# Order of the work between gate and MLP in a fused S5, gate and MLP block on one Trainium2 core

## Chip, cores, metric

One of the cores of a Trainium2 chip runs the whole program; nothing is sent to another core. The metric is device time of one execution in microseconds (us), the median of several runs. TensorE (PE) does the matrix products, VectorE (DVE), ScalarE (ACT) and GpSimd (POOL) the elementwise work, and the queue of SyncE (SP) starts most transfers. Each engine works through its own instructions strictly in program order and waits for the others by semaphores.

## What is computed

One layer on 1024 latent tokens with 1024 channels (and 256 context tokens): modulated RMS norm, a bidirectional state-space mixer, a gate, a second modulated RMS norm, an MLP with squared ReLU, and a last RMS norm. The part at issue begins behind the mixer:

```python
z = gelu(mixer_out)                         # (1024, 1024)
x = x + g1 * (z * sigmoid(z @ glu_w + glu_b))
h = rmsnorm(x, norm2_g) * (1 + sc2) + sh2
a = relu(h @ mlp_w1 + mlp_b1)
x = x + g2 * ((a * a) @ mlp_w2 + mlp_b2)
out = rmsnorm(x, final_g)
```

## The kernel before

**Layout.** Channels lie on the 128 partitions, tokens along the free dimension. The 1024 channels are eight tiles, the 1024 tokens two halves of 512 (`halves`, `hf` 0 and 1). Every operand of a product is kept as two roundings, a high part and a rest (`z[:, 0]`, `z[:, 1]`; the pairs of `put`, `rounded` and `rest`), and a product is three matmuls (`mm3`, L770 to 773). A high part is a copy on ACT (`S.copy`); the rest is a subtraction on DVE or POOL. `T`, `UT`, `W`, `A` and `G2` (`GW`, `G` in the rows) are SBUF tensors; `bank(i)` is a PSUM bank of 512 columns.

**Gate.** `gate(b, d, hf, k)` accumulates eight channel tiles k into the gate of output tile d and half hf. `gate_outs(units, hf, sq, eng, ahead)` (L969 to 981) finishes a list of (tile, bank) units: `z_sum` (L944) adds high part and rest of z on POOL into a buffer, `gate_out` (L949) applies the sigmoid (ACT, L951), multiplies with that buffer (DVE, L952) and adds the result to the residual `acc` (DVE, L953), and `sum_sq` (L960) squares `acc` (ACT, L966) and adds the square to the running sum `ss` (L967; on POOL, or on DVE in the last call). The sums and squares go to buffers that `tmp()` takes in turn from `ring`, seven of the eight `places`; `ahead` says how many z sums are issued in advance.

**First norm.** While the gate of half 1 runs on PE, the norm of half 0 is taken. `norm_cols` (L985) sums `ss` over the partitions on PE (L990) and forms one reciprocal root per token with a root on ACT (L994) between four-element work on DVE (L993 to L1002); `norm_rows` (L1004) spreads it over the partitions on PE (L1008). `norm2` (L1011) then makes z of the second product stage in place: a multiplication (DVE, L1016), scale and shift (ACT, L1017), the high part (ACT, L1024) and the rest (L1027, engine `eng`). Program order at this place: the units (6, 7) of half 0, four `put_w1_half` (ACT L917, DVE L918), the units 0 and 1 of half 1 (L1050), the column sums of the first norm behind the second product of tile 3 (L1056), and the row products behind the second product of tile 4 (L1061). The last call of `gate_outs` (L1069) finishes tiles 2 to 7 of half 1.

**First MLP product.** `h @ w1` is done by seven products instead of eight for each two by two block of quarter operands. `L` lists the 112 products (block b, number i), PE takes them in that order, and `pbank` gives their banks. The operand of the weights is made by `sum1` (L1105; a sum or difference of parts of w1, on POOL for the first blocks), `round1` (ACT, L1111 through L925) and `rest1` (L1115 through L922); for i = 6 `rest1` also starts the load of a later block of w1. `slot(p)` is one of eight slots, so operand p can be rounded only when product p - 8 has read its own. The operand of the tokens is `zop[i]`: quarters of z and the combinations T1, T2, T3, T4, called `t1`, `t2`, `zop[4]` (made in place) and `t4`. PE adds and subtracts quarters with unit matrices into four banks (`z_diff`, L1267), DVE adds more in place (`u2`, L1296 and L1303), and `put` splits them.

`step1(p)` (L1183) issues product p, the first part of what follows it (`after1`, L1150), the rounding of operand p + 5, the output of a finished tile (ACT L1137 and L1138, then a store to DRAM), the rest of operand p + 5 and the sum of operand p + 6; step 0 makes only that last sum. Products 0 to 5 need only half 0 and weights that are ready; the second norm (half 1) lies among them: `norm_cols` behind step 1, `norm_rows` behind step 3, and `norm2_second` ahead of step 5, with its rests on POOL (L1027). So in the program the column sums come behind product 1, product 4 comes behind `norm_rows`, and its copy out of PSUM (ACT, L1160) ahead of the first L1017 of the second norm. Then follow T1, T2, step 6 (with operand 11, the first of the second block), and in one loop over the four tiles T3's split and the two additions that make T4.

The order is written out by hand; each engine's order is the program's.

Of the kernel before, what the change touches and what calls it, by code (L numbers as in the profile page):

```python
# [7 lines left out]
F32 = mybir.dt.float32  # L8
F32R = mybir.dt.float32r
AF = mybir.ActivationFunctionType  # L10
OP = mybir.AluOpType
# [36 lines left out]
def kernel(ctx, tc, cst, bc, x, xl, ada_w, glu_w, w1, w2, out):  # L48
    nc = tc.nc
    V, S, P, PE, SP = nc.vector, nc.scalar, nc.gpsimd, nc.tensor, nc.sync  # L50
# [17 lines left out]
    def vw(ap, *dims):  # L68

        if len(dims) == 1:  # L70
            return ap
        names = "abcdef"[:len(dims)]
        return ap.rearrange("p (%s) -> p %s" % (" ".join(names), " ".join(names)),
                            **{names[i]: dims[i] for i in range(len(dims))})

    def size(dims):
        n = 1
        for d in dims:
            n *= d
        return n  # L80

    def at(tile_, off, *dims):
        return vw(tile_[:, off:off + size(dims)], *dims)

    def sb(off, *dims):
        assert R3 + off + size(dims) <= R3 + NR3
        return at(T, R3 + off, *dims)

    def bank(i, n=512, o=0):
        return PS[:, 512 * i + o:512 * i + o + n]  # L90
# [547 lines left out]
    def slot(i):  # L638
        return CT[:, :, :, 0, i] if i < 14 else LT[:, :, :, 0, i - 14]
# [32 lines left out]
    for q in range(1, 40):  # L672
# [23 lines left out]
        for hf in range(2):  # L696
            p = slot(2 * q - 1)[:, 32 * hf:32 * hf + 32]
# [12 lines left out]
    def zt(j):  # L710
        return vw(zs[j][:, :], 2, 1024)
# [179 lines left out]
    places = [sb(10240 + 512 * i, 512) for i in range(3)] + [at(UT, 512 * i, 512) for i in range(5)]  # L891
    ring = places[:7]
    nt = [0]

    def tmp():
        nt[0] += 1
        return ring[nt[0] % len(ring)]
# [17 lines left out]
    def put(to, src, eng=V, *dims):  # L915
        hi, lo = (vw(v[:, 0:size(dims)], *dims) for v in to) if dims else to
        S.copy(hi, src)  # L917
        eng.tensor_tensor(lo, src, hi.bitcast(F32), op=OP.subtract)  # L918
# [5 lines left out]
    def rounded(to, src, *dims):  # L924
        S.copy(vw(to[0][:, 0:size(dims)], *dims) if dims else to[0], src)  # L925
# [6 lines left out]
    def load_w1(b):  # L932
        SP.dma_start(out=vw(raw1(b), 8, 256), in_=w1v[:, :, 256 * b:256 * b + 256])
# [5 lines left out]
    def put_w1_half(b, kh, p):  # L939
        put(slot(p), vw(raw[0], 2, 2, 4, 128)[:, b % 2, kh], V, 4, 128)  # L940

    zf = {}

    def z_sum(d, hf):  # L944
        z = zt(d).bitcast(F32)
        zf[d, hf] = tmp()
        P.tensor_tensor(zf[d, hf], z[:, 0, halves[hf]], z[:, 1, halves[hf]], op=OP.add)

    def gate_out(b, d, hf):  # L949
        o = acc[:, d, halves[hf]]  # L950
        S.activation(b, b, AF.Sigmoid, bias=C("glub")[:, d:d + 1])  # L951
        V.tensor_tensor(b, zf[d, hf], b, op=OP.mult)  # L952
        V.scalar_tensor_tensor(o, b, g1[:, d:d + 1], o, op0=OP.mult, op1=OP.add)  # L953
# [6 lines left out]
    def sum_sq(d, toks, eng=None):  # L960
        n, ss = toks.stop - toks.start, sq_sum(toks)
        if d == 0:
            S.activation(ss, acc[:, d, toks], AF.Square)
        else:
            sq = tmp()[:, 0:n]
            S.activation(sq, acc[:, d, toks], AF.Square)  # L966
            (eng or P).tensor_tensor(ss, ss, sq, op=OP.add)  # L967

    def gate_outs(units, hf, sq=True, eng=None, ahead=1):  # L969

        for u in units[:ahead]:
            z_sum(u[0], hf)
        for i in range(len(units) + 1):
            if i + ahead < len(units):
                z_sum(units[i + ahead][0], hf)
            if i < len(units):
                gate_out(bank(units[i][1]), units[i][0], hf)
            if units[i:] == [(7, 3)]:
                S.activation(warm, one, AF.Sqrt)
            if i and sq:  # L980
                sum_sq(units[i - 1][0], halves[hf], eng)
# [22 lines left out]
    def norm_rows(r, b, toks=halves[0]):  # L1004

        n = toks.stop - toks.start
        for c in range(n // 128):
            PE.matmul(bank(b, 128, 128 * c), r[:, c:c + 1].to_broadcast([128, 128]), ident, start=True, stop=True)  # L1008
        return bank(b, n)

    def norm2(ds, hf, rb, eng=V):  # L1011
        hs_, xn = halves[hf], {}

        def first(d):
            xn[d] = tmp()
            V.tensor_tensor(xn[d], acc[:, d, hs_], rb, op=OP.mult)  # L1016
            S.activation(xn[d], xn[d], AF.Identity, scale=a2[:, d:d + 1], bias=sh2[:, d:d + 1])  # L1017

        for d in ds[:2]:
            first(d)  # L1020
        for d in ds:
            yield
            z = zt(d)
            S.copy(z[:, 0, hs_], xn[d])  # L1024
            if d + 2 in ds:
                first(d + 2)
            eng.tensor_tensor(z[:, 1, hs_], xn[d], z[:, 0, hs_].bitcast(F32), op=OP.subtract)  # L1027

    def add_b2(hf):
        for d in range(8):  # L1030
# [13 lines left out]
            gate(bank(b), d, 0, k)  # L1044
    gate_outs([(6, 0), (7, 2)], 0)
    G2 = sp.tile([128, 1024], F32, name="G2", tag="gw")
    for p, (b, kh) in enumerate(((0, 0), (1, 0), (0, 1), (1, 1))):
        put_w1_half(b, kh, p)
    load_w1_half(2)
# [7 lines left out]
    for d, b in ((4, 6), (5, 7), (6, 1), (7, 3)):  # L1057
        for k in range(8):
            gate(bank(b), d, 1, k)
            if (d, k) == (4, 1):  # L1060
                rb = norm_rows(r_, 2)  # L1061
# [4 lines left out]
                for kh in range(2):  # L1066
                    put_w1_half(2, kh, 4 + kh)
                load_w1(0)
    gate_outs([(2, 4), (3, 5), (4, 6), (5, 7), (6, 1), (7, 3)], 1, eng=V, ahead=4)  # L1069

# [4 lines left out]
    def zh(k, hf):  # L1077
        z = zt(k)
        return z[:, 0, halves[hf]], z[:, 1, halves[hf]]

    t1, t2, t4 = ([(at(W, o + 1024 * k, 512), at(W, o + 1024 * k + 512, 512)) for k in range(4)] for o in (0, 4096, 8192))
    zop = [[zh(k, 0) for k in range(4)], t1, t2, [zh(4 + k, 1) for k in range(4)], [zh(k, 1) for k in range(4)],
           [zh(4 + k, 0) for k in range(4)], t4]
# [6 lines left out]
    def pbank(p):  # L1090
        return bank((4, 6, 0, 2, 3, 0)[p] if p < 6 else (2, 3, 1, 0, 5, 7, 4, 6)[(p - 6) % 8])
# [3 lines left out]
    def operand(p):  # L1095
        b, i = L[p]
        w = vw(raw1(b), 2, 4, 256)
        a11, a12, a21, a22 = (w[:, kh, :, 128 * f:128 * f + 128] for f in range(2) for kh in range(2))
        s2 = at(G2, 0, 4, 128)
        return (a11, a21, s2, a21, s2, a12, a22)[i], {1: (a21, a22), 2: (a21, a11), 3: (a12, s2), 4: (a22, s2)}.get(i)  # L1100

    def eng1(p):
        return P if p < POS[2, 1] else V

    def sum1(p):  # L1105
        if p < len(L):
            o, ab = operand(p)
            if ab:
                eng1(p).tensor_tensor(o, *ab, op=OP.add if L[p][1] == 1 else OP.subtract)

    def round1(p):  # L1111
        if p < len(L):
            rounded(slot(p), operand(p)[0], 4, 128)

    def rest1(p):  # L1115
        if p < len(L):
            b, i = L[p]
            rest(slot(p), operand(p)[0], eng1(p), 4, 128)
            if i == 6:
                if b == 0:  # L1120
                    load_w1(1)
                elif b < 14:
                    load_w1(b + 2)
                else:
                    load_w2(b - 14)

    def product1(p):
        b, i = L[p]
        hi, lo = (vw(v, 4, 128) for v in slot(p))
        for k in range(4):  # L1130
            mm3(pbank(p), (hi[:, k], lo[:, k]), zop[i][k], k == 0, k == 3)
# [9 lines left out]

    yp = [places[n] for n in (0, 1, 2, 7)] + [at(G2, 512, 512)]

# [37 lines left out]
        yield  # L1181

    def step1(p):  # L1183
        product1(p)
        a = after1(p)
        next(a)
        if p > 0:
            round1(p + 5)
        next(a, 0)
        if p > 0:  # L1190
            rest1(p + 5)
        if p == 7:
            load_w1(2)
        sum1(p + 6)


    UNITS = [[2 * u, 2 * u + 1] for u in range(7)] + [[14], [15]]
# [67 lines left out]
    sums = [bank(i) for i in (5, 7, 4, 6)]  # L1265
# [4 lines left out]
            PE.matmul(sums[k], w, v, start=n == 0, stop=n == 3)  # L1270

    def norm2_second(ks):
        for _ in norm2(ks, 1, rb, P):
            pass

    S.copy(unit[:, 0], ident)
    S.activation(unit[:, 1], ident, AF.Identity, scale=-1.0)
    ring = places[3:7]
    for p in range(6):
        if p == 5:  # L1280
            norm2_second(range(4))
            for k in range(4):
                z_diff(k, zop[4][k], zop[0][k])
            norm2_second(range(4, 8))
            for k in range(4):
                put(t1[k], sums[k])
        step1(p)
        if p == 1:
            r_, *_ = norm_cols(7)
        elif p == 3:  # L1290
            rb = norm_rows(r_, 1)
# [4 lines left out]
            V.tensor_tensor(u2[k], zop[0][k][n].bitcast(F32), u2[k] if n else sums[k], op=OP.add)  # L1296
    for k in range(4):
        put(t2[k], u2[k])
    step1(6)
    for k in range(4):  # L1300
        put(zop[4][k], sums[k])
        for n in range(2):
            V.tensor_tensor(u2[k], zop[5][k][n].bitcast(F32), u2[k], op=(OP.subtract, OP.add)[n])  # L1303
    for k in range(4):
        put(t4[k], u2[k])
    for p in range(7, len(L)):
        b, i = L[p]
# [7 lines left out]
    for u in range(8):  # L1315
        bs = UNITS[u]
        for t in range(16):
            hf, d = t // 8, t % 8
# [45 lines left out]
    ring = ring[:3]  # L1364
# [5 lines left out]
    for d in range(8):  # L1370
# [4 lines left out]
        if d == 5:  # L1375
            rb = norm_rows(r_, 2, first)
# [8 lines left out]
    rb = norm_rows(r_, 3, toks[0])  # L1385
# [12 lines left out]
    rb = norm_rows(r_, 2, toks[1])  # L1398
# [66 lines left out]
```

## Time and profile before

| what | value |
|---|---|
| runs | 1132.06, 1131.56, 1127.25 us; median 1131.56 |
| profiled execution | 1133.16 us, span 1131.4 us |
| PE busy | 988.6 us, 87% of the span |
| DVE, ACT, POOL busy | 779.7, 498.2, 311.8 us |
| TensorE clock granted, mean | 0.936 of full speed |

A busy share is an average over stages with different limits; the stretch of the change lies from 384 to 484 us of the span. A timeline row gives start, length, engine, line, operation, output and inputs, count, and in brackets how long the engine had been idle and what released it.

### The profile page before, as it was taken

The numbers are of one execution on the slowest core, as the hardware profiler recorded it, in microseconds if no ns is written. First come the engines' busy times: TensorE is split into PE (matmuls) and PEld (weight loads), VectorE is DVE, ScalarE is ACT, GpSimd is POOL, SyncE is SP. The second block draws the span as 40 slices with busy tenths as digits, with TensorE's granted clock in tenths as the row PEclk, the third lists the DMA queues.
The fourth block names the chain that finished last, engine by engine and source line by source line (L and its number), as shares of the span: only waits on it lengthen the run. The fifth ranks groups of instructions, "written<-read, shape, count | busy, mean of one in ns | idle before, by whom it ended". The sixth has DMA issues, their size and how long they took to land.

```text
span 1131.4 us, 14742 instructions
## 1 busy us (share of the span) xinstructions
PE 988.6 (87%) x5424; PEld 815.2 (72%) x5424; DVE 779.7 (69%) x1290; ACT 498.2 (44%) x923; POOL 311.8 (28%) x251
## 2 busy tenths in 40 slices
PE   3568676646889997899999999989999999999996
PEld 3337565525878875688888888868888888888885
DVE  8999999999975685775656565656454454454377
ACT  7147474335973566555565655453202202201113
POOL 2787999807562635420000000000000000000003
PEclk9779798867899998899999999999999999999998
DMA  9414355494677410152333232346132232320104
GB/s 383 168 38 147 118 166 136 94 253 133 209 229 243 156 56 19 47 177 99 118 103 119 103 122 103 121 166 243 66 112 90 97 112 75 112 94 19 38 0 149
DMA packets 79032, 142.33 MB, mean 126 GB/s; under 512 B 5744, under 2 KB 44656, under 8 KB 77808
## 3 DMA queue, kind: packets, MB, share of 16 engines
q1 hardware_dynamic: 74528, 126.71, 33.8%
q10 hardware_dynamic: 4432, 14.68, 3.9%
q8 instruction: 42, 0.69, 0.3%
q14 instruction: 30, 0.25, 0.1%
HBM read 106.77 MB, written 34.60 MB: 125 GB/s over the span
## 4 chain that ended last, share of the span: by engine, by line
PE 58%; DVE 23%; DMA 7%; ACT 5%; issue 4%; POOL 2%; SPq 1%; ACTq 0%; DVEq 0%; POOLq 0%
PE PS L771 18%; PE PS L772 18%; PE PS L773 18%; DMA DY<-X 2%; DVE X L468 2%; DVE X L467 2%; DVE PS L466 1%; DVE PS L465 1%; DVE X L449 1%; DVE PS L698 1%; DMA T<-DY 1%; DVE PS L952 1%; DVE UT L700 1%; DVE UT L967 1%; DMA KD<-T 1%
## 5 line engine op out<-in xcount | busy, mean ns | idle before, releaser
L1328 DVE SCALAR_TENSOR_TENSOR T<-PS,T 128x512 f32<-128x512 f32 x128 | 96.1, 751 | 164.5 <-PE PS L773 164.5
L967 POOL TENSOR_TENSOR T<-T,UT 128x256 f32<-128x256 f32 x14 | 10.3, 732 | 620.6 <-DVE T L1000 617.4
L771 PE MATMUL PS<-z,W 128*128 128x512 f32 x400 | 158.5, 396 | 4.1 <-ACT z L917 4.1
L772 PE MATMUL PS<-z,W 128*128 128x512 f32 x400 | 158.8, 397 | 2.8 <-DVE z L918 2.8
L773 PE MATMUL PS<-z,W 128*128 128x512 f32 x372 | 147.1, 395 | 0.0
L772 PE MATMUL PS<-W 128*128 128x512 f32 (+1 forms) x280 | 106.4, 380 | 0.9 <-DVE W L918 0.9
L771 PE MATMUL PS<-W 128*128 128x512 f32 (+1 forms) x280 | 106.6, 381 | 0.0
L773 PE MATMUL PS<-W 128*128 128x512 f32 (+1 forms) x252 | 95.2, 378 | 0.0
L772 PEld LDWEIGHTS PS<-z,W 128*128 128x128 f32 x400 | 76.4, 191 | 20.6 <-DVE z L918 4.8
L771 PEld LDWEIGHTS PS<-z,W 128*128 128x128 f32 x400 | 76.5, 191 | 20.4 <-ACT z L917 4.5
L773 PEld LDWEIGHTS PS<-z,W 128*128 128x128 f32 x372 | 71.3, 192 | 15.1 <-DVE W L823 0.3
L487 PE MATMUL PS<-X,E 128*64 128x160 f32 x256 | 50.8, 341 | 26.5 <-DVE X L449 18.7
L487 PEld LDWEIGHTS PS<-X,E 128*64 128x64 f32 x256 | 35.0, 153 | 38.4 <-issue 21.6
L772 PEld LDWEIGHTS PS<-W 128*128 128x128 f32 x280 | 53.1, 190 | 11.8 <-DVE W L918 2.0
L771 PEld LDWEIGHTS PS<-W 128*128 128x128 f32 x280 | 53.1, 190 | 9.8
L917 ACT CAST W<-UT 128x512 fp32r<-128x512 f32 (+1 forms) x14 | 11.0, 804 | 107.4 <-PE PS L772 99.7
L917 ACT CAST z<-UT 128x1024 fp32r<-128x1024 f32 x8 | 8.1, 1049 | 106.4 <-PE PS L772 106.4
L488 PE MATMUL PS<-X,E 128*64 128x128 f32 x256 | 54.4, 320 | 0.0
L773 PEld LDWEIGHTS PS<-W 128*128 128x128 f32 x252 | 47.7, 189 | 8.7
L1158 DVE TENSOR_TENSOR T<-T,PS 128x512 f32<-128x512 f32 x46 | 31.1, 686 | 32.0 <-PE PS L773 31.4
L773 PE MATMUL PS<-z,A 128*128 128x512 f32 x124 | 48.3, 390 | 0.0
L771 PE MATMUL PS<-z,z 128*128 128x512 f32 x112 | 43.6, 390 | 0.0
(333 smaller groups left out, 2649.4 us busy)
## 6 DMA issues: line engine op xcount, KB each, us to landing
T<-in_w_dram SPq DMA_DIRECT2D x17, 1024.0 KB, 5.4
UT<-in_w_dram SPq DMA_DIRECT2D x15, 1024.0 KB, 5.4
YD<-T SPq DMA_DIRECT2D x36, 256.0 KB, 2.0
T<-in_ada_w_dram ACTq DMA_DIRECT2D x17, 512.0 KB, 4.1
z<-YD SPq DMA_DIRECT2D x32, 256.0 KB, 5.5
W<-YD SPq DMA_DIRECT2D x32, 256.0 KB, 3.5
X<-in_x_dram SPq DMA_DIRECT2D x8, 640.0 KB, 10.1
DX<-X SPq DMA_DIRECT2D x8, 640.0 KB, 3.2
```

Source lines behind the costliest of these rows:

```text
L449: return [lambda: V.tensor_tensor(xv, xv, sc_, op=OP.mult), lambda: V.tensor_tensor(xv, xv, sh_, op=OP.add)]
L467: lambda: eng.tensor_tensor(out_, out_, ta, op=OP.add),
L468: lambda: eng.tensor_tensor(out_, out_, tb_, op=OP.add)]
L487: PE.matmul(b[0:64, c], e[:, g, c, 0:64], uj[:, g], start=True, stop=True)
L488: PE.matmul(b[64:128, c, :, 16:80], e[:, g, c, 64:128], uj[:, g, ::-1, 16:80][:, :, ::-1], start=True, stop=True)
L771: PE.matmul(o, wt[0], xt[0], start=start, stop=False)
L772: PE.matmul(o, wt[0], xt[1], start=False, stop=False)
L773: PE.matmul(o, wt[1], xt[0], start=False, stop=stop)
L917: S.copy(hi, src)
L967: (eng or P).tensor_tensor(ss, ss, sq, op=OP.add)
L1158: V.tensor_tensor(to, x_, o, op=OP.add)
L1328: V.scalar_tensor_tensor(o, bank(t % 8), g2[:, d:d + 1], o, op0=OP.mult, op1=OP.add)
```

## The change

The z sums of tiles 2 to 7 of half 1 are issued behind the last units of half 0, into fixed places, and `ring` has three buffers until the second norm. `gate_outs` has no `ahead` any more and issues the sums that are missing. `norm2` takes a list of engines for its rests: the first norm uses DVE as before, the second DVE for even and POOL for odd tiles. Operands 6 and 7 are made whole ahead of step 0, and operands 8, 9 and 10 in steps 0, 1 and 2, each as sum, rounding and rest in a row; steps 3 and 4 make none, and from step 6 on the old scheme is back (the sum of operand 11 in step 5). T3 is split in a loop of its own ahead of step 6, and T4's additions stay behind it.

```diff
-    def z_sum(d, hf):
+    def z_sum(d, hf, place=None):
-        zf[d, hf] = tmp()
+        zf[d, hf] = tmp() if place is None else place
...
-    def gate_outs(units, hf, sq=True, eng=None, ahead=1):
-        for u in units[:ahead]:
-            z_sum(u[0], hf)
+    def gate_outs(units, hf, sq=True, eng=None):
         for i in range(len(units) + 1):
-            if i + ahead < len(units):
-                z_sum(units[i + ahead][0], hf)
+            for u in units[i:i + 2]:
+                if (u[0], hf) not in zf:
+                    z_sum(u[0], hf)
...
-    def norm2(ds, hf, rb, eng=V):
+    def norm2(ds, hf, rb, eng=(V,)):
...
-            eng.tensor_tensor(z[:, 1, hs_], xn[d], z[:, 0, hs_].bitcast(F32), op=OP.subtract)
+            eng[d % len(eng)].tensor_tensor(z[:, 1, hs_], xn[d], z[:, 0, hs_].bitcast(F32), op=OP.subtract)
...
     gate_outs([(6, 0), (7, 2)], 0)
     G2 = sp.tile([128, 1024], F32, name="G2", tag="gw")
+    ring = places[:3]
+    for d in range(2, 8):
+        z_sum(d, 1, places[1 + d] if d < 6 else at(G2, 512 * (d - 6), 512))
...
-    gate_outs([(2, 4), (3, 5), (4, 6), (5, 7), (6, 1), (7, 3)], 1, eng=V, ahead=4)
+    gate_outs([(2, 4), (3, 5), (4, 6), (5, 7), (6, 1), (7, 3)], 1, eng=V)
...
         next(a)
-        if p > 0:
+        if p > 5:
             round1(p + 5)
         next(a, 0)
-        if p > 0:
+        if p < 3:
+            operand1(8 + p)
+        elif p > 5:
             rest1(p + 5)
         if p == 7:
             load_w1(2)
-        sum1(p + 6)
+        if p > 4:
+            sum1(p + 6)
+
+    def operand1(p):
+        sum1(p)
+        round1(p)
+        rest1(p)
...
-        for _ in norm2(ks, 1, rb, P):
+        for _ in norm2(ks, 1, rb, (V, P)):
...
     ring = places[3:7]
+    for p in (6, 7):
+        operand1(p)
     for p in range(6):
...
     for k in range(4):
         put(t2[k], u2[k])
+    for k in range(4):
+        put(zop[4][k], sums[k])
     step1(6)
     for k in range(4):
-        put(zop[4][k], sums[k])
         for n in range(2):
             V.tensor_tensor(u2[k], zop[5][k][n].bitcast(F32), u2[k], op=(OP.subtract, OP.add)[n])
```

## Rows read from the trace of the kernel before

**Rows 1.** Windows, PE: stretch, length, busy (instructions), granted clock, DMA, GB/s.

```profile
400.10:401.20 1.10, 0.01 (x1) 1.00 0.02 5
...
432.40:437.90 5.50, 5.48 (x17) 0.50 0.00 0
...
448.40:455.00 6.60, 6.02 (x13) 0.50 0.01 2
...
500.00:750.00 250.00, 250.00 (x1104) 1.00 0.34 115
```

**Rows 2.** Timeline of PE, 400 to 484 us.

```profile
401.19 1.16 PE L1008 MATMUL PS<-T 128*128 128x128 f32 x8 [1.13 <-DVE T L1002]
...
432.42 1.87 PE L990 MATMUL PS<-T,UT 128*128 128x1 f32 x8 [4.20 <-DVE UT L967]
...
441.49 1.05 PE L1008 MATMUL PS<-T 128*128 128x128 f32 x8
...
448.42 0.79 PE L1270 MATMUL PS<-z,W 128*128 128x512 f32 x1 [3.12 <-ACT z L1024]
...
473.76 0.50 PE L772 MATMUL PS<-z,W 128*128 128x512 f32 x1 [1.57 <-DVE z L918]
...
483.44 0.40 PE L771 MATMUL PS<-W 128*128 128x512 f32 x1
```

**Rows 3.** Timeline of POOL, 386 to 459 us.

```profile
386.34 2.54 POOL L947 TENSOR_TENSOR UT<-z 128x512 f32<-128x512 f32 x2
...
392.65 1.73 POOL L947 TENSOR_TENSOR T<-z 128x512 f32<-128x512 f32 x1
...
414.84 1.29 POOL L967 TENSOR_TENSOR UT<-UT 128x512 f32<-128x512 f32 x1 [18.76 <-ACT UT L966]
...
433.59 1.27 POOL L922 TENSOR_TENSOR A<-T,A 128x512 fp32r<-128x512 f32 x1 [6.89 <-ACT A L925]
...
436.82 1.28 POOL L922 TENSOR_TENSOR A<-G,W 128x512 fp32r<-128x512 f32 x1 [0.73 <-ACT W L925]
...
448.44 10.03 POOL L1027 TENSOR_TENSOR z<-UT,z 128x512 fp32r<-128x512 f32 x8 [0.66 <-ACT z L1024]
```

**Rows 4.** Timeline of DVE, 391 to 433 us.

```profile
391.79 5.43 DVE L918 TENSOR_TENSOR W<-T,W 128x512 fp32r<-128x512 f32 x4 [1.26 <-ACT W L917]
397.15 0.68 DVE L952 TENSOR_TENSOR PS<-T,PS 128x512 f32<-128x512 f32 x1
...
399.93 0.15 DVE L993 TENSOR_SCALAR T<-PS 128x4 f32<-128x4 f32 x1
...
418.30 0.68 DVE L952 TENSOR_TENSOR PS<-UT,PS 128x512 f32<-128x512 f32 x1
...
426.85 0.68 DVE L967 TENSOR_TENSOR UT<-UT,T 128x512 f32<-128x512 f32 x1
...
428.84 0.68 DVE L967 TENSOR_TENSOR UT<-UT,T 128x512 f32<-128x512 f32 x1
...
431.67 0.69 DVE L967 TENSOR_TENSOR UT<-UT 128x512 f32<-128x512 f32 x1 [0.16 <-ACT UT L966]
```

**Rows 5.** Timeline of ACT, 431 to 470 us.

```profile
431.01 0.63 ACT L966 ACTIVATE UT<-T 128x512 f32<-128x512 f32 x1 [0.77 <-DVE T L953]
...
434.52 0.21 ACT L994 ACTIVATE T<-T 128x4 f32<-128x4 f32 x1 [1.01 <-DVE T L993]
...
446.34 1.52 ACT L1017 ACTIVATE UT<-UT,T 128x512 f32<-128x512 f32 x2
...
468.88 0.62 ACT L925 CAST W<-T 128x512 fp32r<-128x512 f32 x1 [3.10 <-POOL T L1109]
469.40 2.04 ACT L917 CAST z<-PS 128x512 fp32r<-128x512 f32 x4
```

**Rows 6.** Timeline of DVE, 456 to 483 us.

```profile
456.75 2.48 DVE L918 TENSOR_TENSOR W<-PS,W 128x512 fp32r<-128x512 f32 x4 [2.58 <-ACT W L917]
...
478.80 3.57 DVE L918 TENSOR_TENSOR W<-UT,W 128x512 fp32r<-128x512 f32 x4
```

## Prediction, made before the changed kernel was run

> **What bounds the kernel now.** I read the windows first. From 500 to 750 us PE is busy in all of the 250 us, at full clock, with a product about every 0.226 us [rows 1], and this goes on to the end of the MLP but for one pause between its two products, which the change leaves alone. So what the change wins or loses ahead of the dense part is kept to the end; the station at which I take the balance is the first product of operand 11, at 483.44 us [rows 2]. PE's timeline ahead of it shows the pauses: 1.13 us ahead of the row products of the first norm (401.19), 4.20 ahead of the column sums of the second (432.42), 3.12 ahead of the first unit product (448.42), and about 10 us of halting products from 473.76, where product 9 waits for T3's rests [rows 2]. The windows add the clock: the idle 1.1 us left the granted clock at 1.00, but the idle 4.20 and 3.12 were followed by 5.5 and 6.6 us at 0.50, the lower of its two levels, 1.2 GHz [rows 1, 2]. Dense work loses half of such a stretch: 2.75 us for 5.5.
>
> **Sums of z ahead of the first norm.** The change takes four sums from ahead of the last gate call and two from inside it, and puts all six on POOL behind the last square of half 0. There POOL has next the sums of units 0 and 1, which began at 392.65 [rows 3]. After them POOL sat idle for 18.76 us [rows 3], so there is room; but the order counts. In the new program the six stand *ahead* of the sums of units 0 and 1, DVE needs these for L952 at 397.15, and the whole first norm (L993 at 399.93) is queued behind L952 on DVE [rows 4].
>
> A sum costs 1.27 us where POOL is alone (two in 2.54) and 1.73 beside DVE's four rests of w1 [rows 3]; those cost 1.36 each there (5.43 for four), where a comparable DVE operation has 0.68 [rows 4]. I take three of the six at 1.73 and three at 1.27, 9.0 us, because the four rests end near 397.2. The six end at 401.65, the sum of unit 0 at 402.9, and L952 comes 402.9 - 397.15 = 5.7 us later; unit 1's sum is ready when DVE has done unit 0. The ends are six at 1.27 (4.4 us later) and all at 1.73 (7.6). POOL and DVE thus seem to take turns. The Trainium skill (SBUF — State Buffer, section "SBUF: two separate sides") gives the rule: the two share a port pair that one instruction holds to its end, a DVE operation with two SBUF inputs included; by that the sum is 5.7, without it 4.4. The rule speaks against this part of the change, and the trace agrees (1.73 against 1.27).
>
> So L1008 moves from 401.19 to 406.9 and PE's pause from 1.13 to 6.8 us. That is longer than both pauses that were followed by the low clock, so I add 2.75 us (ends: 0, as after 1.13 us, and 3.3, half of 6.6). PE was through with product 1 at 432.42 - 4.20 = 428.2 [rows 2]; now at 428.2 + 5.7 + 2.75 = 436.7.
>
> **The last gate call.** DVE's chain began at 418.30 and ended at 432.36, 14.1 us for six units [rows 4]. Its pace with no sum beside it is 1.99 us a unit (426.85 to 428.84), so six take 11.9, with the wait for the last square 12.2; one sum of w1 on POOL may block one square, 0.9 more. It starts 5.7 later, and 0.7 for L1008 at half clock: 424.7, and ends at 436.9 to 437.8. PE arrives at 436.7: its pause of 4.20 shrinks to 1.1 at most, and the low clock behind it goes. The column sums start near 437.4 (432.42 before); the path from there to the second L1008 was 9.1 us [rows 2], at full clock it is about 6.4 (1.0 for the sums, 24 products of 0.226), so PE is there at 443.8 instead of 441.49.
>
> **Operands ahead of their products.** What is late next is the root of the second norm. It (ACT L994, 434.52) stands in ACT's queue behind step 1, and the roundings of operands 6 to 9 now stand ahead of it. Each rounding waits for POOL's sum, which waits for the rest before: 433.59 to 436.82, 3.23 us per operand [rows 3], made of one rounding (0.62) and two POOL operations. ACT is through with the last square of the gate as DVE's last addition begins (431.01 + 0.63 = 431.64, addition 431.67 [rows 4, 5]), now about 436.6. With 0.4 for the two unit matrices the first rounding starts at 437.0, the fourth at 446.7, the root at 447.4, 12.9 later than before. From L993 to L1008 it took 1.26 us in the first norm [rows 2, 4], so L1008 comes at 448.5, 7.0 later than 441.49, and PE, there at 443.8, stands for 4.7 us. That is again above 4.20, so the clock falls: L1008 and product 4 take some 2.0 us longer (ends 0 and 2.75). The copy of product 4 stands ahead of L1017 on ACT, so L1017 moves from 446.34 [rows 5] to 455.3: 9.0 later. Slots are no obstacle: operands 8 to 10 wait for products 0 to 2, which are done. Operand 10's rest issues the second block's load on SP earlier than before; that transfer has then time enough. The roundings that are gone from steps 3 and 4 cost nothing and gain nothing, since ACT waits there.
>
> **Rests on two engines.** POOL took 10.03 us for eight, 1.25 each [rows 3]; ACT needs about the same per tile (446.34 to the T1 casts ahead of 456.75, eight tiles [rows 5, 6]), so the rests had little to give: 0.35 us on the first four. DVE's multiplications for tiles 3 to 7 now queue behind its own rests, which wait for ACT. I count 1.6 us later for T1's rests (ends -0.5, the whole gain of a quicker last rest, and +2.5, two waits for ACT).
>
> **T3 ahead of T4.** Before, ACT's casts for T3 (469.40) stood behind the rounding of operand 11, which waited 3.10 us for POOL [rows 5]; now they follow T2's. Counting DVE from L1017: T1's rests at 10.4 [rows 5, 6] + 1.6 = 12.0, then four rests 2.5, one output 0.7, eight additions for T2 at 0.68, 5.4, four rests of T2 and four of T3, 5.0, eight additions for T4 5.4 and 1.0 for POOL beside them: 32.0, first rest of T4 done at 32.7. Product 10 then has 11 products, 2.5: 35.2. Before it was 483.44 - 446.34 = 37.1 [rows 2, 5]. The gain is 2 us: the halting product 9 goes, but product 7 waits for T2 (some 3 us) and product 10 for T4. If the clock falls only at product 10, the gain is lost (-0.7); that is its lower end, 2.5 the upper.
>
> **Sum.** L1017 9.0 later, 2.0 back: 7.0 us slower. The profiled execution took 1133.16 us, 1.6 above the median of 1131.56, so it would be 1140.2 there and 1138.6 as a median. A measurement of this kernel can tell about 0.5%, 5.7 us, from no change.
>
> **Rivals.**
> *POOL's queue does not hold the first norm* (the sums of units 0 and 1 come first after all, so that the change doesn't do what its order says). For it: POOL's 18.76 idle us, and DVE only needs the six at 418.30. Against: POOL runs in order. Then DVE's chain ends near 430.5, the roundings start at 430.6, the root comes at 441.0 and L1008 at 442.1, 0.6 later; low clock +2.0, behind L1017 -2.0: 1132, no change.
> *POOL is quicker than its rows here*, the one way to the other side. At DVE's 0.68 per operation the six sums take 4.1 us, the first norm is 0.3 late, and the rounding chain has 2.0 us per operand, so that the root is ready when PE comes. Then the pause of 4.20 shrinks by 2 and loses its 2.75 of low clock, and T3 brings 2: about 1125. It decides below some 0.8 us an operation; all POOL rows of this size have 1.25 or more, so I give it little.
> *The clock falls everywhere*: all at the upper ends, sums at 1.73, and a pause at product 10 of its own: 1.9 + 0.6 + 0.7 + 2.0 more, 1143 to 1144.
>
> **Numbers.** Forecast 0.62, with its own range of 1134 to 1142 (sums 4.4 to 7.6, clock 0 to 3.3); no change by POOL's order 0.18; faster 0.08; clock everywhere 0.12. Two thirds of the forecast lies above 5.7 us: slower 0.41 + 0.12 = 0.53, same 0.21 + 0.18 = 0.39, faster 0.08. The range of 1130 to 1143 leaves out the faster case and the outer parts of the no-change case and the last one.
>
> **What would show it.** Right: six L947 in a row from 392.65; DVE L952 waiting for POOL's L947 some 5.7 us; L1008 near 407 behind an idle 6 to 7 us, then a window at 0.50; less than 1.5 us ahead of L990; L994 near 447 behind four roundings, a second L1008 with 4 to 5 us of idle ahead; no wait of product 9 for L918, but waits of products 7 and 10. Wrong: the first L1008 before 403, or the second without a pause; and if product 11 starts before 485, the forecast is wrong whatever its steps show.

## The result, and the profile after

The changed kernel takes 1138.16 us (median of five runs, 1137.21 to 1141.96), the kernel before, run beside it, 1130.63 (1126.56 to 1132.06): a ratio of 1.0083, 95% interval 1.0054 to 1.0113. It is slower by 0.8%; the forecast was 1138.6. The profiled run of after took 1138.16 us with a span of 1136.4, that of before 1133.16 and 1131.4, so the two traces show 5.0 us of the 7.5 between the medians. PE is busy for 989.3 us of the span, 87%.

In the profile of after everything ahead of the stretch runs 0.67 us later (the first column sums begin at 394.18, before at 393.51). Where a time of after is set against one of before, this is taken off and the difference is called corrected. The lines of the helpers moved by a few: L1007 is the row products that were L1008, L989 the column sums (L990), L992 and L993 the first operation of the norm and its root (L993, L994), L1016 the multiplication on ACT (L1017), L1281 the unit products (L1270), L1111 the sums of w1 (L1109).

The timeline of POOL in after shows where the six sums stand; the answer to it before is [rows 3].

```profile
393.29 6.83 POOL L947 TENSOR_TENSOR UT<-z 128x512 f32<-128x512 f32 x4
...
400.08 2.49 POOL L947 TENSOR_TENSOR G<-z 128x512 f32<-128x512 f32 x2
402.54 2.48 POOL L947 TENSOR_TENSOR T<-z 128x512 f32<-128x512 f32 x2
...
441.54 1.28 POOL L922 TENSOR_TENSOR A<-G,W 128x512 fp32r<-128x512 f32 x1 [0.73 <-ACT W L925]
```

Four sums into UT, beside DVE's rests, take 1.71 each, two into G 1.25 each; only then do the two for units 0 and 1 begin. The timeline of DVE in after shows who waits for them [rows 4 and 6 before]:

```profile
392.44 6.53 DVE L918 TENSOR_TENSOR W<-T,W 128x512 fp32r<-128x512 f32 x4 [1.26 <-ACT W L917]
...
403.82 0.70 DVE L952 TENSOR_TENSOR PS<-T,PS 128x512 f32<-128x512 f32 x1 [4.85 <-POOL T L947]
...
406.61 0.15 DVE L992 TENSOR_SCALAR T<-PS 128x4 f32<-128x4 f32 x1
...
425.77 0.70 DVE L952 TENSOR_TENSOR PS<-UT,PS 128x512 f32<-128x512 f32 x1 [0.51 <-ACT PS L951]
...
448.10 0.18 DVE L995 RECIPROCAL T<-T 128x4 f32<-128x4 f32 x1 [8.42 <-ACT T L993]
...
466.01 2.48 DVE L918 TENSOR_TENSOR W<-PS,W 128x512 fp32r<-128x512 f32 x4 [0.31 <-ACT W L917]
...
485.30 3.57 DVE L918 TENSOR_TENSOR W<-UT,W 128x512 fp32r<-128x512 f32 x4
```

DVE stands 4.85 us for POOL ahead of L952 and later 8.42 us for the root on ACT. The L952 at 425.77 begins the last gate call, 466.01 are T1's rests and 485.30 T4's. ACT's timeline shows what stands ahead of that root [rows 5]: four roundings (L925), the later ones with a wait of over 2 us for POOL's next sum. The last two rows are T3's casts and, now behind them, the rounding of operand 11.

```profile
437.63 0.60 ACT L925 CAST A<-T 128x512 fp32r<-128x512 f32 x1
440.85 0.62 ACT L925 CAST W<-G 128x512 fp32r<-128x512 f32 x1 [2.61 <-POOL G L1111]
444.09 0.62 ACT L925 CAST W<-T 128x512 fp32r<-128x512 f32 x1 [2.14 <-POOL T L1111]
447.34 0.62 ACT L925 CAST W<-G 128x512 fp32r<-128x512 f32 x1 [2.15 <-POOL G L1111]
447.86 0.20 ACT L993 ACTIVATE T<-T 128x4 f32<-128x4 f32 x1
...
454.21 1.52 ACT L1016 ACTIVATE UT<-UT,T 128x512 f32<-128x512 f32 x2
...
474.94 2.04 ACT L917 CAST z<-PS 128x512 fp32r<-128x512 f32 x4
476.86 0.65 ACT L925 CAST W<-T 128x512 fp32r<-128x512 f32 x1
```

PE's timeline has the pauses in brackets [rows 2], and PE's windows the granted clock [rows 1]. The pause at 475.04 is that of product 7, the one at 486.05 that of product 10, and 490.25 is the start of product 11.

```profile
407.87 2.07 PE L1007 MATMUL PS<-T 128*128 128x128 f32 x8 [7.14 <-DVE T L1001]
...
438.11 1.37 PE L989 MATMUL PS<-T,UT 128*128 128x1 f32 x8 [1.56 <-DVE UT L967]
...
449.77 1.16 PE L1007 MATMUL PS<-T 128*128 128x128 f32 x8 [1.83 <-DVE T L1001]
...
475.04 0.50 PE L772 MATMUL PS<-W 128*128 128x512 f32 x1 [1.40 <-DVE W L918]
...
486.05 0.50 PE L772 MATMUL PS<-W 128*128 128x512 f32 x1 [2.55 <-DVE W L918]
...
490.25 0.39 PE L771 MATMUL PS<-W 128*128 128x512 f32 x1
```

```profile
407.00:413.00 6.00, 5.13 (x19) 0.64 0.00 0
...
438.00:440.00 2.00, 1.89 (x10) 0.67 0.00 0
440.00:444.00 4.00, 4.00 (x11) 0.50 0.00 0
...
449.00:451.00 2.00, 1.23 (x10) 1.00 0.00 0
...
486.00:488.00 2.00, 1.96 (x6) 0.62 0.00 0
```

The first product of operand 11 begins at 490.25, before at 483.44: 6.8 us later, 6.1 corrected. From there on both kernels run the same dense work. By the end of these two profiled runs 1.8 of the 6.8 are given back: the pause between the two products of the MLP is 3.72 us (4.12 before), and the stretch at 0.50 behind it lasts some 3.5 us, before some 6.5, which brings the last norm's column sums to 5.3 us behind those of before (1119.07 against 1113.74).

### The profile page after: what moved, and what is told of

Its sections match the earlier page's. It is cut to its first block, busy times and chain, and to the rows that moved or that the text cites. A ratio compares the mean times of both kernels' runs of the same rounds, so it can differ in the third digit from the quotient of the medians.

```text
span 1136.4 us, 14738 instructions
## 1 busy us (share of the span) xinstructions
PE 989.3 (87%) x5424; PEld 816.5 (72%) x5424; DVE 779.2 (69%) x1294; ACT 499.2 (44%) x923; POOL 306.2 (27%) x247
## 4 chain that ended last, share of the span: by engine, by line
PE 56%; DVE 26%; ACT 6%; DMA 5%; issue 3%; POOL 3%; SPq 1%; ACTq 0%; DVEq 0%; POOLq 0%
PE PS L772 18%; PE PS L773 18%; PE PS L771 18%; DVE X L468 2%; DMA DY<-X 2%; DVE X L467 2%; DVE PS L466 2%; DVE PS L465 2%; DVE X L449 1%; DMA T<-DY 1%; DVE PS L698 1%; ACT T L723 1%; SPq L583 1%; POOL UT L967 1%; ACT T L722 1%
## 5 line engine op out<-in xcount | busy, mean ns | idle before, releaser
L490 ACT COPY X<-PS 128x264 f32<-128x264 f32 x64 | 24.5, 383 | 44.0 <-PE PS L489 30.4
## 6 DMA issues: line engine op xcount, KB each, us to landing
X<-in_x_dram SPq DMA_DIRECT2D x8, 640.0 KB, 10.4
```

Of the source, the lines that this page charges most:

```text
L490: S.copy(LT[:, 8 * j + g], b[:, :, ::-1, 14:80])
```

## The experiments

Theory, after the result: the loss has two places of one kind. A queue that serves in order was given work that is needed late ahead of work that is needed soon: POOL's six sums hold the first norm, and ACT's roundings hold the root of the second. The rival to it: the two are side effects, and the time is lost to contention between POOL and DVE or to PE's low clock wherever the sums and roundings stand.

Each run is set against runs of the kernel before on the same chip. As the profiles differ by up to 5.5 us ahead of this stretch, one table gives stations in us after the start of the first column sums of the same profile: the first row products, the second column sums, the second row products, the first L1016 (L1017 before), and the first product of operand 12, just behind the halting products.

```
                        row 1   col 2   row 2   L1016   op. 12   ratio [95%]
before                   7.68   38.91   47.98   52.83   92.67
after                   13.69   43.93   55.59   60.03   98.79   1.0083 [1.0054, 1.0113]
units first             10.93   41.24   52.91   59.70   98.48   1.0043 [1.0027, 1.0060]
sums only               13.70   43.95   52.02   56.86   97.21   1.0049 [1.0035, 1.0063]
operands only            7.68   38.91   50.59   56.46   94.57   1.0018 [1.0005, 1.0031]
T3 only                  7.96   39.19   48.05   52.90   91.15   0.9996 [0.9984, 1.0009]
rests only               7.66   38.89   48.13   52.98   95.41   1.0016 [1.0005, 1.0027]
root first              10.91   41.21   49.33   54.54   93.38   1.0004 [0.9993, 1.0016]
root first, POOL rests  11.18   41.50   47.97   54.86   92.26   0.9999 [0.9983, 1.0015]
no early sums            7.67   38.91   48.09   52.42   89.23   0.9970 [0.9956, 0.9984]
T2's rests on POOL       7.65   38.88   47.99   52.32   89.64   0.9982 [0.9969, 0.9994]
sums behind product 2    7.62   38.85   43.88   48.51   86.35   0.9945 [0.9926, 0.9964]
sums behind product 3    7.61   39.93   44.90   47.08   84.94   0.9931 [0.9915, 0.9948]
```

**Units first.** The changed kernel, with the sums of units 0 and 1 ahead of the six.

```diff
+    for d in range(2):
+        z_sum(d, 1)
     for d in range(2, 8):
         z_sum(d, 1, places[1 + d] if d < 6 else at(G2, 512 * (d - 6), 512))
```

> The changed kernel with one thing moved: the z sums of units 0 and 1 of half 1 are issued on POOL ahead of the six sums of units 2 to 7. Theory (the six hold the first norm, and that is carried to the end): L952 of unit 0 comes without a wait for POOL, the first row products at about 401 us instead of 407.9, the column sums near 430.6, the root behind four roundings near 440.6, and the time is 5 to 8 us below the changed kernel, within 2 us of the kernel before. Rival (the delay of the first norm is absorbed, because PE stood 4.2 us ahead of the column sums anyhow, and the loss is made later by roundings and split rests): the time is at most 2 us below the changed kernel.

It took 1135.64 us against 1130.90, ratio 1.0043: a third of the loss went by the medians, half by the ratios, less than expected. DVE's timeline of this run, and a row of POOL's:

```profile
399.18 0.68 DVE L952 TENSOR_TENSOR PS<-T,PS 128x512 f32<-128x512 f32 x1
...
402.38 0.18 DVE L995 RECIPROCAL T<-T 128x4 f32<-128x4 f32 x1 [0.27 <-ACT T L993]
...
402.91 1.18 DVE L999 TENSOR_TENSOR T<-T 128x4 f32<-128x4 f32 x1
404.13 1.18 DVE L1001 SCALAR_TENSOR_TENSOR T<-T 128x4 f32<-128x4 f32 x1
```

```profile
402.82 2.47 POOL L947 TENSOR_TENSOR G<-z 128x512 f32<-128x512 f32 x2
```

L952 no longer waits for its sum, but the row products come only 2.8 us sooner than in after, still 3.25 later than before. All four of DVE's rests (L918) now run beside POOL and take 6.52 us, before 5.43, so that L952 comes 1.1 later. And the six sums now run beside the first norm: two of its five operations on four elements take 1.18 us each, where the same ones have 0.17 in the first norm of the kernel before. Each ends as one of POOL's two sums into G ends. That makes the other 2.1. The Trainium skill (SBUF — State Buffer, section "SBUF: two separate sides") states that a DVE operation with two SBUF inputs and a POOL operation that reads SBUF take turns on a shared port pair, and that the loser is blocked for the whole instruction of the other. The rows agree: L999 and L1001 read two SBUF operands and are held, the reciprocal reads one and takes 0.18 beside the same sums. They also show that the held operation may be tiny. So the rival has a share in the sums' cost: of the 6.0 us by which the six sums move the first row products, their order makes 2.8 and the contention beside them the other 3.2. In the second norm nothing is gained: the roundings hold the root as before, PE waits 5.00 us ahead of the row products, and the low clock behind them eats the rest.

```profile
447.00:453.00 6.00, 5.65 (x18) 0.55 0.20 62
```

**Each part alone**, added to the kernel before: the sums, then the operands, T3 and the split rests. Their diffs are the four parts of the change's own diff; together they are the changed kernel.

> The kernel before with the first part of the change alone: six z sums ahead of those of units 0 and 1, into fixed places. Theory: first row products near 407, column sums near 437.5, nothing new behind them, so 3 to 7 us slower than before. Rival (absorbed): 0 to 2 us slower.

> The kernel before with the operands alone moved ahead of their products (operands 6 and 7 ahead of step 0, 8 to 10 in steps 0 to 2). Theory: the root stands behind four roundings at a pace of 3.2 us, near 442.5 instead of 434.5, and PE stands about 3 us ahead of the second row products; on the other side the rounding of operand 11 no longer waits for its load, so T3's casts come 2 to 3 us earlier: in all -1 to +3 us against the kernel before. Rival (this part makes the whole loss): 5 to 8 us slower.

> The kernel before with T3's split alone moved ahead of step 6 and of T4's additions. Theory: T3's casts no longer stand behind the rounding of operand 11, product 9 does not halt, DVE loses its wait of 2.5 us there: 1 to 3 us faster than before. Rival (the wait only moves to T4): within 0.5 us of the kernel before.

> The kernel before with the rests of the second norm alone split over DVE and POOL. Theory: ACT sets the pace there, and DVE's multiplications now queue behind its own rests, so T1's rests come 1 to 1.5 us later behind the first L1017 than the 10.4 us of before: 0.5 to 2.5 us slower. Rival (two engines finish the rests sooner): 0 to 2 us faster.

Measured: sums 1136.25 (1.0049), operands 1132.93 (1.0018), T3 1130.12 (0.9996, no measurable difference) and rests 1133.95 (1.0016), against 1130.90 and for the rests 1130.85. At operand 12 the sums cost 4.54 us, the operands 1.90 and the rests 2.74, and T3 gives 1.52: 7.7 in sum, 6.1 when all are together, so they overlap a little. The parts' ratios add up to 0.79%, all at once cost 0.83%.

The operands alone hold the root and the row products behind it: the root comes 48.7 us after the first column sums, before 41.0. The first row is ACT's timeline, the second PE's:

```profile
443.10 0.20 ACT L994 ACTIVATE T<-T 128x4 f32<-128x4 f32 x1
```

```profile
445.01 1.23 PE L1008 MATMUL PS<-T 128*128 128x128 f32 x4 [3.46 <-DVE T L1002]
```

T3 alone removes the halts of product 9 and makes product 10 wait, with the low clock behind (0.50 from 481 to 483); the gain at operand 12 is 1.5 us, and the time does not show it. The expected 1 to 3 us were not measured. PE's timeline of this run:

```profile
479.02 0.50 PE L772 MATMUL PS<-W 128*128 128x512 f32 x1 [3.39 <-DVE W L918]
```

The split rests cost on DVE's own queue: a multiplication of the norm waits behind a rest that waits for ACT, so T1's rests begin 11.8 us after the first L1017 (446.91), where before it was 10.4 [rows 5, 6]. DVE's timeline:

```profile
451.65 0.69 DVE L1027 TENSOR_TENSOR z<-UT,z 128x512 fp32r<-128x512 f32 x1 [1.39 <-ACT z L1024]
...
457.72 0.69 DVE L1027 TENSOR_TENSOR z<-UT,z 128x512 fp32r<-128x512 f32 x1 [1.39 <-ACT z L1024]
458.72 2.48 DVE L918 TENSOR_TENSOR W<-PS,W 128x512 fp32r<-128x512 f32 x4 [0.31 <-ACT W L917]
```

**Root first.** "Units first", with operands 8 and 9 issued behind the root of the second norm rather than ahead of it.

```diff
-        if p < 3:
-            operand1(8 + p)
+        if p == 2:
+            operand1(10)
...
             r_, *_ = norm_cols(7)
+            operand1(8)
+            operand1(9)
```

> The run with the sums of units 0 and 1 first, and in it operands 8 and 9 made behind the column sums and the root of the second norm instead of ahead of them. Theory (four roundings hold the root): root near 439.5 instead of 445.4, no pause and no low clock at the second row products, first L1017 near 447 instead of 454, so 4 to 6 us below that run, about level with the kernel before. Rival (that stage is late because the first norm is late and the clock low): within 2 us of that run.

1132.33 against 1130.85, ratio 1.0004, level with before; below "units first" it lies 3.3 us by the medians and 4.4 by the ratios, where 4 to 6 were expected. The root comes at 439.40 instead of 445.44 and PE has no pause ahead of the second row products. So the order in ACT's queue, not the roundings' work, cost this part: the same operands are made.

**Root first, rests on POOL.** The same with `norm2(ks, 1, rb, (P,))`.

> The run with the root first (six early sums behind those of units 0 and 1, operands 8 and 9 behind the root, T3 ahead), and in it the rests of the second norm on POOL alone again. Theory (the split of the rests costs 1 to 3 us wherever it stands, by DVE's multiplications waiting behind its own rests): 1 to 3 us below that run, 1129 to 1131.5 us. Rival (the split only lost in the kernel before, where nothing else was moved): within 0.7 us of that run.

1130.65 against 1131.12, ratio 0.9999. Below "root first" that is 1.7 us by the medians, as the theory has it, but 0.6 by the ratios, as the rival has it, and the intervals overlap: this run does not decide between them. That the split costs time is shown by "rests only" alone.

The table shows one thing more. The second row products come as early as before (47.97), yet L1016 comes 2.0 later. ACT's roundings of operands 8 to 10 and two outputs stand ahead of product 4's copy, on which L1016 waits, and the chain of sums and roundings begins when the gate ends, here 2.6 us later than before: product 4 ends near 446.7, and its copy begins at 449.20. Behind the root, too, the operands are free only if the gate ends in time.

**No early sums.** The kernel before with operands and T3 as in the last run, its sums of z left where they were.

> The kernel before (its z sums and its rests on POOL) with operands 6, 7 ahead of step 0, 8 and 9 behind the root, 10 in step 2, and T3 ahead of step 6. Theory: no part that lost is left; the root comes near 436.5, still ahead of PE, and T3 and operand 11 wait for nothing, but PE then waits for T4: 0.5 to 2.5 us faster than before. Rival (operands ahead lose in any place, by POOL beside DVE's norm): 1 to 3 us slower.

1127.88 against 1130.85, ratio 0.9970: faster than both kernels. What is left of the change is good; the sums in a row and the split rests are not.

From "root first, POOL rests" this run differs by the early sums alone, and it is 2.8 us below it by the medians, 3.3 by the ratios. So the sums cost some 3 us even where units 0 and 1 come first and the root stands ahead of operands 8 and 9: order is not the whole of their price.

In its profile the clock has a share in this. Product 10 waits as long as in after (2.53 us against 2.55), but here the clock stays at 1.00 behind it. PE's timeline and windows of this run:

```profile
472.98 0.50 PE L772 MATMUL PS<-W 128*128 128x512 f32 x1 [2.53 <-DVE W L918]
```

```profile
473.00:475.00 2.00, 2.00 (x9) 1.00 0.00 0
```

From the first L1017 to operand 12 this run takes 36.81 us; "root first, POOL rests", with the same program there, the same pause (2.54) and the low clock behind it, takes 37.40 and the kernel before 39.84.

**T2's rests on POOL**, to free DVE for T4.

```diff
-        put(t2[k], u2[k])
+        put(t2[k], u2[k], P)
```

> The run without early sums, and T2's four rests on POOL instead of DVE. Theory (PE waits in products 7 and 10 for DVE's row of additions and rests): DVE has 2.5 us less ahead of T3 and T4, T2's first rest comes some 2.5 us earlier, product 7 hardly waits, and the time is 1.5 to 3.5 us below that run. Rival (POOL and DVE take turns, and DVE's additions wait for POOL's rests): within 1 us of that run, or slower.

1128.96 against 1130.85, ratio 0.9982: no gain over "no early sums", as the rival had it. POOL's and DVE's timelines of this run:

```profile
460.79 6.38 POOL L918 TENSOR_TENSOR W<-UT,W 128x512 fp32r<-128x512 f32 x4 [2.36 <-ACT W L917]
```

```profile
463.70 1.08 DVE L1309 TENSOR_TENSOR UT<-z,UT 128x512 f32<-128x512 f32 x1
...
468.35 7.15 DVE L1317 TENSOR_TENSOR UT<-z,UT 128x512 f32<-128x512 f32 x8
```

A rest costs POOL 1.6 us here, and DVE's eight T4 additions beside it take 7.15 us, 6.28 in "no early sums": what DVE hands over it pays back.

**Column sums behind product 2, behind product 3** ("sums behind product 2" and "3" in the table). "No early sums" still has the pause of 4.20 ahead of the second column sums with the low clock behind it. Here that matmul group is issued one and two products later, which lets PE work while DVE ends the gate, and operands 7 to 10 stand behind the root. The first of the two, against "no early sums":

```diff
-    for p in (6, 7):
-        operand1(p)
+    operand1(6)
...
-        if p == 2:
-            operand1(10)
-        elif p > 5:
+        if p > 5:
...
                 put(t1[k], sums[k])
+            round1(9)
+            rest1(9)
+            operand1(10)
         step1(p)
-        if p == 1:
+        if p == 2:
             r_, *_ = norm_cols(7)
+            operand1(7)
             operand1(8)
-            operand1(9)
+            sum1(9)
```

The second has `p == 3` there and the row products at `p == 4`, and another buffer for one output of product 3, whose old place the norm still uses:

```diff
-        y11 = p11 if b > 2 else yp[4 - b % 2]
+        y11 = p11 if b > 2 else places[5] if b == 1 else yp[4 - b % 2]
```

> The run without early sums, and in it the column sums of the second norm one product later, behind product 2, with the roundings of operands 7 and 8 behind the root and those of 9 and 10 behind T1's. Theory (PE's pause of 4.2 us ahead of the column sums and the low clock behind it are what is left to win in this stage): PE fills the pause with product 2, the pause shrinks to about 1.5 us, the second row products come some 3 to 5 us earlier against the first column sums, and the time is 2 to 5 us below the run without early sums. Rival (DVE's chain sets the norm, so the row products come no earlier, and later roundings lose): within 1 us of it.

> As the run before it, but the column sums behind product 3 and the row products behind product 4. Theory: PE has no pause there and stays at full clock up to the row products, which come near 437 (before: 441.5, against first column sums at 393.5); 3 to 7 us below the run without early sums. Rival (DVE's chain sets the norm): within 1 us of it.

1123.85 (0.9945) and 1123.15 us (0.9931) against 1131.12, 4.0 and 4.7 below "no early sums" by the medians (2.8 and 4.4 by the ratios), both within what was expected. Between the two the runs do not tell. The last beats both kernels: 0.7% under before and, by the two ratios (0.9931 / 1.0083 = 0.985), 1.5% under after. Its PE timeline and windows:

```profile
432.99 0.95 PE L990 MATMUL PS<-T,UT 128*128 128x1 f32 x8
...
437.96 1.16 PE L1008 MATMUL PS<-T 128*128 128x128 f32 x8 [1.14 <-DVE T L1002]
```

```profile
434.00:436.00 2.00, 2.00 (x10) 1.00 0.24 89
```

The column sums have no pause ahead and the clock behind them is full. Of the 7.7 us won at operand 12 against before, 5.75 stand already at the first L1016 (47.08 against 52.83). How much the later column sums win by themselves, without the later operands, was not tried: in "no early sums" product 4 ends and ACT is through with its roundings and outputs at the same time (441.8), which speaks for both being needed.

## Why the prediction was right, and which of its steps were not

The forecast, that the time would grow by about 7 us, held, and for the reason given; two steps of its sum failed, a third term was too large, and their errors partly cancel.

- *Six sums on POOL.* Forecast 9.0 us, measured 9.3 (393.29 to 402.57); L952 5.7 later, measured 6.0 corrected; PE's pause 6.8, measured 7.14. "Units first" shows that a change of order alone wins 2.8 of the 6.0 back, and why not all: the sums then hold two of the norm's small operations and all four rests. The prediction had reckoned with POOL and DVE taking turns only for the large operations.
- *The low clock behind that pause.* It came (0.64 over 407 to 413), and product 1 ended at 435.9 corrected, forecast 436.7: 435.9 less 428.2 and the 6.0 of the later start leaves 1.7 us for it, not 2.75.
- *The last gate call.* 12.3 us from L952 to the end of its last addition, forecast 12.2 to 13.1; the column sums at 437.4 corrected, as forecast.
- *Failed: "the low clock behind it goes".* The prediction let the pause ahead of the column sums shrink to 1.1 us at most and took the clock behind it for full. It was 1.56, and 440 to 444 had 0.50. PE reached the second row products at 447.3 corrected, not 443.8. It cost nothing in the sum, because the root was later still.
- *Roundings ahead of the root.* Four roundings with POOL's steps between them, root at 447.2 corrected, forecast 447.4. "Operands only" against before (root 48.7 us after the first column sums against 41.0) and "root first" show it as the cause.
- *Failed: the low clock at the second row products.* With PE 3.5 later than forecast, its pause was 1.83 rather than 4.7, and the clock behind it stayed at 1.00. So the 2.0 us for that were not paid. Beside it, the path from the root to the row products took 1.9 us, not 1.1, as L997 (two SBUF inputs) took 1.00 beside POOL (the same operation, L998, has 1.14 in the second norm of the kernel before); and 0.4 was won behind them, where no rounding stands between product 4's copy and L1016 any more. In all L1016 came 7.2 corrected later, not 9.0.
- *Rests on two engines.* T1's rests 11.8 us after the first L1016, forecast 12.0; "rests only" confirms this chain and that the part alone costs time (1.0016).
- *T3 ahead of T4, mis-sized.* Product 9 ran through, products 7 and 10 waited, as forecast; but the clock fell at product 10 (0.62), which the prediction held for the lower end. In "no early sums", with a wait of 2.53 us against 2.55, it did not fall. The gain from L1016 to operand 11 was 1.06 us, not 2.0. "T3 only" has a like wait (3.39 us) and no measurable gain.

The sum: 7.2 later less 1.06, 6.1 corrected, forecast 7.0. That the medians differ by 7.5 and the profiled runs by 5.0 is within the spread of the runs (before alone covers 5.5 us), so the nearness of 1138.16 to 1138.6 is in part luck. Of the rivals, POOL's order holds the norm after all; no POOL operation of this size in the stretch took less than 1.24 us; and the clock did not fall everywhere.

Open: a place for the six sums at which POOL is idle and DVE has neither large nor small operations to hold was not tried. Nor was it tried whether T4's rests can be made before product 10 asks for them.

## What to carry to other kernels

Idle time on an engine is no licence to send it work early: in a queue that serves in order, ask what stands behind the new work and who waits for that, here the two sums of the first norm and one root of 0.2 us. Where work for a later need must be placed, put it behind the short operation on which another engine waits; the same operands cost time ahead of the root and none behind it in "no early sums", where the gate ends as early as before. Ask also what runs beside the work that is moved: with the order mended, the early sums still cost some 3 us. And before making a wait shorter, look whether the waiting step can be issued later instead: eight short matmuls behind two more products, together with later operands 7 to 10, won 4.7 us.

## What the runs showed of the hardware beyond that

The length of a pause did not by itself say whether the clock falls. Ahead of the second column sums, eight matmuls with one column each, pauses of 0.89 ("sums only"), 0.90 ("root first"), 1.48 ("sums behind product 2") and 1.56 us (after) were all followed by a stretch at or near 0.50, while 0.43 ("units first"), 0.45 ("root first, POOL rests") and none at all ("sums behind product 3") were not. Yet 1.83 us ahead of the second row products in after, eight matmuls of 128 columns, left it at 1.00. There the work on both sides differs. Ahead of product 10 it does not: dense products of 512 columns stand on both sides, and pauses of 2.48 ("root first"), 2.54 ("units first" and "root first, POOL rests") and 2.55 us (after) were followed by some 3 us at 0.50, while 2.52 ("T2's rests on POOL") and 2.53 ("no early sums") left it at 1.00. So pauses of the same length amid the same work went both ways, each in one profiled execution; what decides was not isolated.

POOL holds even DVE's smallest operations, where these have two SBUF inputs: 1.18 us for one of 0.17. For the large ones the price is on both sides: a sum of 128 x 512 on POOL has 1.25 alone and 1.71 beside DVE's rests, and four rests on DVE have 6.53 beside POOL, 2.48 alone.
